# One diffusion-transformer step on one core: where the rows of the MLP norm come from, and which token tiles are paired for the MLP's operands

## The chip, the cores and the metric

The kernel runs on one core of one Trainium2 chip. The metric is device time in microseconds, median of three runs. PE is the matmul engine (TensorE), PEld its weight load, DVE VectorE, ACT ScalarE, POOL GpSimd, SP SyncE; all DMAs of this kernel are issued by SP, on one queue.

## The reference

One layer over 17 token tiles of 128 tokens: tile 0 is the context (128 tokens), tiles 1 to 16 are the latent tokens (2048). D is 1024, the MLP is 4096 wide.

```python
def block(x, s0, mod, ...):
    sh1, sc1, ga1, sh2, sc2, ga2 = mod
    h = rmsnorm(x, norm_mix_l) * (1.0 + sc1) + sh1
    o, s_new = mixer(h, s0, ...)          # projections, two-way delta scan, gMLP, w_out
    x = x + ga1 * o
    h = rmsnorm(x, norm_ffn_l) * (1.0 + sc2) + sh2
    x = x + ga2 * (jnp.square(jax.nn.relu(h @ w_ff1_l)) @ w_ff2_l)
    return x, s_new
```

The block runs once for the context (with `c_ctx`) and once for the latent tokens (with `c`); a last RMSNorm follows. The change is about the second norm: from `x` after the mixer to the operands of `h @ w_ff1_l`. All arithmetic is float32: each matmul operand is split into a rounded high part and a low part, and three matmuls make one product (`mm3`, lines 213 to 219).

## The kernel before

There are four stages in order of time: projections and convolution (to about 450 us); the scans over 34 units of one tile and direction (to about 1320); the first MLP matmul (to about 2370); the second.

**The backward scan** is a list of events with times in units (one unit is one tile's scan step). For tile t at unit i, `o_steps` (from line 1238) ends with the projection by w_out, adds the residual into two SBUF tiles `u["x"]` (lines 1293 to 1295), and stores them to the DRAM tensor `x2_d` (line 1296). Tiles 16 to 9 then run `h2_steps` (line 799) here, at offsets 3.17 to 3.71 (norm and transposes) and 3.71 to 4.71 (operands) from the list `WINDOWS`.

**`h2_steps(t)`** gives a list of steps:
- `norm2`: loads the tile's rows from `x2_d` (line 809), squares them on ACT with a running sum (811), DVE adds the sums, `rsqrt_cols` takes DVE and then POOL (175, 176), DVE scales the rows (815).
- `trans2(half)`: four PE transposes (822), then ACT applies the modulation (825) into `ev`; tiles named in `h2_d` are stored to DRAM (828).
- Tiles 4 to 1 and 12 to 9 go on: `partner` loads the stored `ev` of tile t + 4 as `y` (836), and `plain`, `third`, `fifth`, `sixth`, `fourth` form seven operands from the quarters of the pair (a fast 2 x 2 block scheme with seven products; the differences are line 849). `put` splits each into high part (ACT, 843) and low part (DVE, 844) and stores both to `hop_d` (846).

**The first MLP matmul** has two halves, g = 0 for tiles 9 to 16 and g = 1 for tiles 1 to 8 and 0. A half has 16 units of 256 hidden columns; a unit has seven products (`ORDER` = 1, 5, 6, 7, 3, 2, 4), and each product (a "step", position p in `seq`) is 12 matmuls of 512 columns against a resident operand tile (`hop`, 1 MB). Units 0 and 1, 14 and 15, 16 and 17 are interleaved product by product. In g = 1 tile 0's products come in as 128-column matmuls. With 112 steps in the first half, position 112 (`half`) starts the second.

At each p the program asks, in this order, for: the raw weights of the unit of step p + 10 (`loads_at(p + LEAD + 4)`, line 1445, four DMAs of 256 KB); the split weights of step p + 6 (`weights_at`, lines 1415 and 1421, made on DVE and ACT); the steps of `later` that are due; the products and their results (`step`, from line 1486), which ACT or DVE takes out of PSUM and SP stores to `z_d` (1481) and `s1_d`, `s2_d` (1484). `later` holds the `h2_steps` of tiles 8 to 0, 51 steps from p = 8 on at even distances of 90/51 = 1.76. `first_tile` (at p = 104) loads tile 0's `h2_d` (1554) and splits it right away on ACT and DVE. `hop_next` (893) loads the next operand tile; at p = 99, 101, ..., 111 (each step of unit 15) it loads one for the second half, into the buffer whose last reader is that step.

**Buffers and order.** Most tiles of 512 columns come from one pool `wp` of 49 (`w512`). The framework orders each engine's instructions by program order and by a planner's own model of time, hands out buffers as they come free in that model, and puts in the waits. At run time each engine, SP too, works its list in that order and stops at the first instruction whose wait isn't met.

Of the kernel before, what the change touches and what calls it, by code (L numbers as in the profile page):

```python
# [8 lines left out]
F32 = mybir.dt.float32  # L9
# [8 lines left out]
P = 128  # L18
# [43 lines left out]
def hybrid_step(  # L62
# [17 lines left out]
    def cond(t):  # L80
        return 0 if t == 0 else 1
# [20 lines left out]
    gate_d = dp.tile([NTOK, 512], F32, name="gate_d")  # L102
    ob_d = dp.tile([NTOK, 512], F32, name="ob_d")
    x2_d = dp.tile([NTOK, D], F32, name="x2_d")
    h2_d = {t: dp.tile([P, KT, P], F32, name=f"h2_{t}_d") for t in (0, 5, 6, 7, 8, 13, 14, 15, 16)}
    hop_d = {(g, o): dp.tile([P, 4, 2, 512], F32, name=f"hop_{g}_{o}_d") for g in range(2) for o in range(1, 8)}
    z_d = [dp.tile([4 if a else 1, P, 2, NK, P], F32, name=f"z{a}_d") for a in range(5)]
    s1_d, s2_d = ([dp.tile([4, P, NK, P], F32, name=f"s{i}{g}_d") for g in range(2)] for i in (1, 2))
# [95 lines left out]
    def w512(name):  # L204
        return wp.tile([P, 512], F32, tag="w", name=name)

    def wrow(row):

# [587 lines left out]

    bs = vec[:, 69:73]

    def h2_steps(t, psum, tmp, wide=w512):

        u = {}
        cd = cond(t)

        def norm2():
            u["x"] = x = [wide("x"), wide("x")]
            ss = smp.tile([P, 2], F32, tag="ss2", name="ss2")
            r = smp.tile([P, 1], F32, tag="r", name="r")
            for n in range(2):
                load(out=x[n], in_=x2_d[t * P : (t + 1) * P, n * 512 : (n + 1) * 512])
                junk = tmp()  # L810
                A.activation(junk, x[n], AF.Square, accum_out=ss[:, n : n + 1])
            V.tensor_tensor(out=ss[:, 0:1], in0=ss[:, 0:1], in1=ss[:, 1:2], op=ALU.add)
            rsqrt_cols(r, ss[:, 0:1], 1, 1.0 / D, EPS)
            for n in range(2):
                V.tensor_scalar_mul(x[n], x[n], r)

        def trans2(half):
            def f():
                ps = psum()
                ev = wide("ev")  # L820
                for i in range(4):
                    T.transpose(ps[:, i * P : (i + 1) * P], u["x"][half][:, i * P : (i + 1) * P], ident)
# [10 lines left out]
        def partner():  # L833
            u["y"] = [wide("y"), wide("y")]
            for half, y in enumerate(u["y"]):
                load(out=y.rearrange("p (k d) -> p k d", k=4), in_=h2_d[t + 4][:, half * 4 : half * 4 + 4, :])

        def put(o, src):

            dst = hop_d[t <= 8, o][:, :, :, (t - 1) % 4 * P : (t - 1) % 4 * P + P]  # L840
            h = wp.tile([P, 512], F32R, tag="w", name="opH")
            lo = wp.tile([P, 512], F32R, tag="w", name="opL")
            A.copy(h, src)
            V.tensor_tensor(out=lo, in0=src, in1=f32(h), op=ALU.subtract)
            for i, part in enumerate((h, lo)):
                store(out=dst[:, :, i, :], in_=f32(part).rearrange("p (k d) -> p k d", k=4))

        def sub(a, b, out=None):
            V.tensor_tensor(out=a if out is None else out, in0=a, in1=b, op=ALU.subtract)

        def plain():
            put(1, u[0])
            put(2, u[1])

        def third():
            put(3, u["y"][1])
            d = wide("d")
            sub(u["y"][1], u["y"][0], d)
            put(7, d)

        def fifth():
            sub(u["y"][0], u[0])
            put(5, u["y"][0])

        def sixth():
            sub(u["y"][1], u["y"][0])
            put(6, u["y"][1])

        def fourth():
            sub(u[1], u["y"][1])  # L870
            put(4, u[1])

        ops = [] if t in h2_d else [partner, plain, third, fifth, sixth, fourth]
        return [norm2, trans2(0), trans2(1)] + ops

    def sraw():
        return sp.tile([P, 512], F32, tag="raw", name="sraw")
# [18 lines left out]
    with ExitStack() as ph:  # L896
# [321 lines left out]
        def fraw():  # L1218
            return fp.tile([P, 512], F32, tag="gw", name="fraw")


        WO = []

# [14 lines left out]
        def o_steps(du):  # L1238
# [41 lines left out]
            def proj(n, k0):  # L1280
                def f():
                    if k0 == 0:
                        u["ps"] = pj()
                    for k in (k0, k0 + 1):
                        mm3(u["ps"], [(u["H"][k], u["L"][k]) + WO[n][k]], first=k == 0,
                            last=k == KT - 1)
                    if k0 == KT - 2:
                        sl = slice(n * 512, (n + 1) * 512)
                        tmp = fp.tile([P, 512], F32, tag="ug" if n else "vg", name="tmp")
                        ga = ga1[n]  # L1290
                        if cond(t) == 0:
                            ga = wrow(mod_d[0:1, 2 * D + n * 512 : 2 * D + n * 512 + 512])
                        x = u["x"][n]
                        V.tensor_tensor(out=tmp, in0=u["ps"], in1=ga, op=ALU.mult)
                        V.tensor_tensor(out=x, in0=x, in1=tmp, op=ALU.add)
                        store(out=x2_d[t * P : (t + 1) * P, sl], in_=x)
                return f

# [35 lines left out]
        for i, u in enumerate(units):  # L1334
            w = p2 if i <= NT else p3
            at(i - 3 if i > PL else -10, u["prep_loads"])
            at(i - 1, u["scan_loads"])
            n = len(u["prep"])
            for j, st in enumerate(u["prep"]):
                at(i - w[0] + (j + 0.5) * (w[0] - w[1]) / n, st, "prep")  # L1340
            spread(i + w[2], i + w[3], [scan_step(i, f) for f in u["scan"]], "chain")
            if i in (0, NT):
                at(i + w[2] + (w[3] - w[2]) * 0.7, lambda i=i: after(i))
            if i >= NT:
                at(i, lambda u=u: o_loads(u))
                first, second = o_steps(u)
                spread(i + p3[4], i + p3[5], first, "fill")
                spread(i + p3[6], i + p3[7], second, "fill")
                if u["t"] > 8:
                    st = h2_steps(u["t"], pj, fraw)  # L1350
                    spread(i + p3[8], i + p3[9], st[:3], "fill")
                    spread(i + p3[9], i + p3[9] + 1, st[3:], None)
        f2 = [f2_steps(t) for t in range(NT)]
        flat = []
        for n, (t, gi) in enumerate([(t, "g") for t in range(HT)] + [(t, gi) for t in range(HT) for gi in "vu"]
# [76 lines left out]
    class Unit:  # L1432
# [45 lines left out]
                first=onto is None, more=onto is not None)  # L1478

        def out(self, i, th, z):  # L1480
            store(out=z_d[(4, 2)[self.g] - 1 + th][:, :, i, self.jp, :].rearrange("a p d -> p a d"), in_=as4(z))

        def keep(self, dst, z):
            store(out=dst[self.g][:, :, self.jp, :].rearrange("a p d -> p a d"), in_=as4(z))
# [72 lines left out]
            x0[1].append(lo)  # L1557


    pairs = [(9 + i, 13 + i) for i in range(4)] + [(1 + i, 5 + i) for i in range(4)]  # L1560
    y0 = {}
    acc = {}
    kept = {}
# [56 lines left out]
    def s_parts(i, u, q):  # L1620

        ks = slice(4 * q, 4 * q + 4)

        def z(t, h):
            return z_d[(t + 3) // 4][(t - 1) % 4 if t else 0, :, h, ks, :]

        if u == 8:
            return {1: lambda: ([z(0, 0)],), 7: lambda: ([z(0, 0)],), 3: lambda: ([z(0, 0), z(0, 1)], ALU.add),
                    2: lambda: ([z(0, 1)],)}[i]()
        a, b = pairs[u]  # L1630
        g, m = divmod(u, 4)
        return {1: lambda: ([z(a, 0)],),
                5: lambda: ([s1_d[g][m, :, ks, :]],),
                6: lambda: ([s2_d[g][m, :, ks, :]],),
                7: lambda: ([z(a, 0), z(b, 0)], ALU.subtract),
                3: lambda: ([z(a, 1), s2_d[g][m, :, ks, :]], ALU.subtract),
                4: lambda: ([z(b, 1)],),
                2: lambda: ([z(a, 1)],)}[i]()
# [125 lines left out]
            begun.add(seq[p][1])  # L1764
            units[seq[p][1]].loads()

    for p in range(LEAD):
        loads_at(p)
    for p in range(LEAD):
        if p < 5:  # L1770
            hop_next()
        weights_at(p)
    later = [st for t in range(8, -1, -1) for st in h2_steps(t, bank, lambda: w512("junk"), w512)]
    n0 = len(seq) // 2 - 14
    later = [(8 + j * (n0 - 16) // len(later), st) for j, st in enumerate(later)]
    half = [p for p, e in enumerate(seq) if e[1] == NP][0]
    last = len(seq) - 16
    ps0 = None
    for p, (o, n, b) in enumerate(seq):
        u = units[n]  # L1780
        loads_at(p + LEAD + 4)
        weights_at(p + LEAD)
        while later and later[0][0] <= p:
            later.pop(0)[1]()
        if p == half - 8:
            first_tile()
        if o:
            u.step(o)
        if u.g:
# [108 lines left out]
```

## Time and profile before

| what | value |
|---|---|
| median of three runs (lowest, highest) | 2788.17 us (2787.95, 2789.26) |
| profiled execution | 2800.44 us |
| its span | 2798.7 us |
| its mean granted TensorE clock | 0.977 |
| DMA traffic | 585.10 MB, mean 209 GB/s |
| chain that ended last | PE 75%, DMA 10%, DVE 9%, issue 2%, ACT 2% |

In profile lines, `out<-in` names the tiles, `xN` is a count, L217 to L219 are the three matmuls of `mm3`, and a bracket at a line's end is the engine's idle time before the instruction and what ended it. A line of the waits reads: who waited, for whom, us in total, times, longest. The granted clock is the share of full speed that the chip allowed TensorE; 0.50 is half speed.

### The profile page before, as it was taken

The numbers are of one execution on the slowest core, as the hardware profiler recorded it, in microseconds if no ns is written. First come the engines' busy times: TensorE is split into PE (matmuls) and PEld (weight loads), VectorE is DVE, ScalarE is ACT, GpSimd is POOL, SyncE is SP. The second block draws the span as 40 slices with busy tenths as digits, with TensorE's granted clock in tenths as the row PEclk, the third lists the DMA queues.
The fourth block names the chain that finished last, engine by engine and source line by source line (L and its number), as shares of the span: only waits on it lengthen the run. The fifth ranks groups of instructions, "written<-read, shape, count | busy, mean of one in ns | idle before, by whom it ended". The sixth has DMA issues, their size and how long they took to land.

```text
span 2798.7 us, 45208 instructions
## 1 busy us (share of the span) xinstructions
PE 2655.7 (95%) x15698; PEld 2209.5 (79%) x15698; DVE 1869.1 (67%) x3909; ACT 1246.6 (45%) x3092; POOL 232.7 (8%) x448
## 2 busy tenths in 40 slices
PE   8999998999999899899798887999999999999998
PEld 4999996778887777778677776888888787788887
DVE  5867656777777878775467664655565555775874
ACT  4655555555555567653344442223342341332441
POOL 3111113111111111100000000000000000000000
PEclk9999999999999999899999898999999999999999
DMA  8866649555455667884758667433459997876682
GB/s 288 272 196 211 194 145 279 169 151 167 147 170 166 200 201 242 267 255 169 249 163 235 177 206 275 121 107 114 119 158 308 336 330 239 305 228 228 220 258 97
DMA packets 571691, 585.10 MB, mean 209 GB/s; under 512 B 35948, under 2 KB 401948, under 8 KB 567878
## 3 DMA queue, kind: packets, MB, share of 16 engines
q1 hardware_dynamic: 571462, 582.22, 65.4%
q8 instruction: 123, 2.02, 0.3%
q14 instruction: 106, 0.87, 0.1%
HBM read 402.34 MB, written 179.74 MB: 208 GB/s over the span
## 4 chain that ended last, share of the span: by engine, by line
PE 75%; DMA 10%; DVE 9%; issue 2%; ACT 2%; SPq 1%; POOL 1%; DVEq 0%; POOLq 0%; ACTq 0%
PE f L217 14%; PE f L219 14%; PE f L218 14%; PE pj L217 6%; PE pj L219 5%; PE pj L218 5%; PE pd L943 2%; DMA x<-x_d 2%; DMA qT<-qT_d 2%; PE pm L217 1%; PE pm L219 1%; PE pm L218 1%; PE pd L1120 1%; PE pt L568 1%; PE pd L1121 1%
## 5 line engine op out<-in xcount | busy, mean ns | idle before, releaser
L217 PE MATMUL f<-hop,wH 128*128 128x512 f32 x896 | 361.1, 404 | 52.6 <-ACT x L1491 21.6
L219 PE MATMUL f<-hop,zL 128*128 128x512 f32 x960 | 377.0, 393 | 1.8 <-DVE zL L1415 1.8
L217 PE MATMUL f<-hop,zH 128*128 128x512 f32 x960 | 376.7, 393 | 1.9 <-ACT zH L1421 1.9
L218 PE MATMUL f<-hop,zH 128*128 128x512 f32 x960 | 377.0, 393 | 0.0
L218 PE MATMUL f<-hop,wH 128*128 128x512 f32 x896 | 355.9, 397 | 0.0
L219 PE MATMUL f<-hop,wL 128*128 128x512 f32 x896 | 355.3, 397 | 0.0
L1421 ACT CAST zH<-zraw 128x512 fp32r<-128x512 f32 x240 | 147.0, 620 | 292.6 <-DVE zraw L1415 85.8
L217 PEld LDWEIGHTS f<-hop,wH 128*128 128x128 f32 x896 | 171.8, 192 | 90.7 <-ACT x L1491 22.4
L217 PEld LDWEIGHTS f<-hop,zH 128*128 128x128 f32 x960 | 180.4, 188 | 45.5 <-ACT zH L1421 2.7
L219 PEld LDWEIGHTS f<-hop,zL 128*128 128x128 f32 x960 | 180.3, 188 | 44.9 <-DVE zL L1415 2.6
L218 PEld LDWEIGHTS f<-hop,zH 128*128 128x128 f32 x960 | 180.2, 188 | 40.9
L1415 DVE TENSOR_TENSOR zL<-zraw,zH 128x512 fp32r<-128x512 f32 x240 | 162.8, 687 | 70.8 <-ACT zH L1421 54.2
L219 PEld LDWEIGHTS f<-hop,wL 128*128 128x128 f32 x896 | 171.5, 191 | 38.9
L218 PEld LDWEIGHTS f<-hop,wH 128*128 128x128 f32 x896 | 172.0, 192 | 35.8
L217 PE MATMUL pj<-kH,wH 128*128 128x386 f32 (+2 forms) x568 | 190.6, 338 | 0.3 <-DVE kH L466 0.3
L219 PE MATMUL pj<-kH,wL 128*128 128x386 f32 (+2 forms) x568 | 190.2, 335 | 0.0
L218 PE MATMUL pj<-kL,wH 128*128 128x386 f32 (+2 forms) x568 | 189.5, 334 | 0.0
L176 POOL TENSOR_TENSOR r<-rsq,nhalf 128x1 f32<-128x1 f32 (+1 forms) x38 | 26.3, 692 | 1575.4 <-DVE rsq L175 1575.4
L1415 DVE TENSOR_TENSOR wL<-raw,wH 128x512 fp32r<-128x512 f32 x112 | 76.4, 688 | 80.3 <-ACT wH L1421 79.3
L516 DVE SCALAR_TENSOR_TENSOR cv<-pj,vec,cv 128x384 f32<-128x384 f32 (+2 forms) x164 | 87.2, 539 | 59.4 <-ACT cv L513 57.9
L217 PEld LDWEIGHTS pj<-kH,wH 128*128 128x128 f32 x568 | 107.2, 189 | 4.9 <-issue 4.4
L217 PE MATMUL pj<-wH,hH 128*128 128x512 f32 x248 | 110.4, 445 | 0.0
(398 smaller groups left out, 6117.0 us busy)
## 6 DMA issues: line engine op xcount, KB each, us to landing
zraw<-z_d SPq DMA_DIRECT2D x212, 256.0 KB
raw<-in_w_ff_dram SPq DMA_DIRECT2D x128, 256.0 KB
hop<-hop_d SPq DMA_DIRECT2D x28, 1024.0 KB
z_d<-c SPq DMA_DIRECT2D x96, 256.0 KB
zraw<-s_d SPq DMA_DIRECT2D x96, 256.0 KB
raw<-in_w_mod_dram SPq DMA_DIRECT2D x80, 256.0 KB
r<-in_w_ff_dram SPq DMA_DIRECT2D x80, 256.0 KB
x<-x_d SPq DMA_DIRECT2D x68, 256.0 KB
```

The costliest lines, as they stand in the source:

```text
L176: G.tensor_tensor(out=out, in0=t[:np_, :n], in1=nhalf[:np_, :n], op=ALU.pow)
L217: T.matmul(ps, lh, rh, start=first and i == 0, stop=False, skip_group_check=more)
L218: T.matmul(ps, lh, rl, start=False, stop=False, skip_group_check=more)
L219: T.matmul(ps, ll, rh, start=False, stop=last and i == n - 1, skip_group_check=more)
L516: V.scalar_tensor_tensor(out=cv[:, o : o + m], in0=ps[:, s + sh : s + sh + m], scalar=convw[:, w, j : j + 1], in1=cv[:, o : o + m], op0=AL ...
L568: T.matmul(ps[:, i * P : (i + 1) * P], kTt[:, i * P : (i + 1) * P], rhs[:, i * P : (i + 1) * P], start=True, stop=True)
L943: T.matmul(p[:, h, :], lhs[:, h, :], rhs[:, h, :], start=True, stop=True)
L1120: T.matmul(p[:, h, :], u["qT"][:, h, :], s[:, h, :], start=True, stop=False)
L1121: T.matmul(p[:, h, :], u["QK"][:, h, :], u["vn"][:, h, :], start=s is None, stop=True)
L1415: V.tensor_tensor(out=out, in0=a, in1=b, op=op)
L1421: A.copy(h, src)
```

## The change

1. In `h2_steps`, loading (`rows`), `squares`, the reciprocal root (`norm2`) and scaling (`scale2`) become steps of their own. The partner's load moves into `squares`.
2. For tiles 8 to 0 `rows` is placed three steps ahead of the tile's position p = 10 + 19j/2 (j = 0 for tile 8), and the k-th further step at p + k. So rows are asked for at p - 3, squares come at p + 1, transposes at p + 4 and p + 5, operands of odd tiles at p + 6 to p + 10.
3. For tiles 16 to 9 there are no `rows`: `squares` takes the SBUF tiles that `o_steps` made. The offsets become 3.17 to 3.91, and 3.91 to 5.81 for operands.
4. Pairs are (t, t + 1) with t odd, where they were (t, t + 4). Operands are made for 15, 13, 11, 9 and 7, 5, 3, 1. The layouts of `hop_d`, `z_d` and `pairs` follow.
5. In the scan, `y` and `d` come from a new pool of five, the high and low parts from the four `raw` staging buffers.
6. Raw weights are asked for at p + 14 where it was p + 10; `first_tile` moves from 104 to 102; `hop_next` from 99, 101, ..., 111 to 101, 103, ..., 113.

```diff
-    h2_d = {t: dp.tile([P, KT, P], F32, name=f"h2_{t}_d") for t in (0, 5, 6, 7, 8, 13, 14, 15, 16)}
+    h2_d = {t: dp.tile([P, KT, P], F32, name=f"h2_{t}_d") for t in range(0, NT, 2)}
...
-    def h2_steps(t, psum, tmp, wide=w512):
+    def h2_steps(t, psum, tmp, wide=w512, part=None, half=None, src=None):
...
+        wide, part, half = wide, part or wide, half or w512
+
+        def rows():
+            u["x"] = [wide("x"), wide("x")]
+            for n in range(2):
+                load(out=u["x"][n], in_=x2_d[t * P : (t + 1) * P, n * 512 : (n + 1) * 512])
+
+        def squares():
+            if src:
+                u["x"] = src()
+            u["ss"] = smp.tile([P, 2], F32, tag="ss2", name="ss2")
+            for n in range(2):
+                A.activation(tmp(), u["x"][n], AF.Square, accum_out=u["ss"][:, n : n + 1])
+            if t % 2:
+                u["y"] = [part("y"), part("y")]
+                for h, y in enumerate(u["y"]):
+                    load(out=y.rearrange("p (k d) -> p k d", k=4), in_=h2_d[t + 1][:, h * 4 : h * 4 + 4, :])
 
         def norm2():
-            u["x"] = x = [wide("x"), wide("x")]
...
+            u["r"] = smp.tile([P, 1], F32, tag="r", name="r")
+            V.tensor_tensor(out=u["ss"][:, 0:1], in0=u["ss"][:, 0:1], in1=u["ss"][:, 1:2], op=ALU.add)
+            rsqrt_cols(u["r"], u["ss"][:, 0:1], 1, 1.0 / D, EPS)
+
+        def scale2():
             for n in range(2):
-                load(out=x[n], in_=x2_d[t * P : (t + 1) * P, n * 512 : (n + 1) * 512])
...
+                V.tensor_scalar_mul(u["x"][n], u["x"][n], u["r"])
...
-            dst = hop_d[t <= 8, o][:, :, :, (t - 1) % 4 * P : (t - 1) % 4 * P + P]
-            h = wp.tile([P, 512], F32R, tag="w", name="opH")
-            lo = wp.tile([P, 512], F32R, tag="w", name="opL")
+            c = (t - 1) % 8 // 2 * P
+            dst = hop_d[t <= 8, o][:, :, :, c : c + P]
+            h, lo = half("opH", F32R), half("opL", F32R)
...
-        ops = [] if t in h2_d else [partner, plain, third, fifth, sixth, fourth]
-        return [norm2, trans2(0), trans2(1)] + ops
+        ops = [plain, third, fifth, sixth, fourth] if t % 2 else []
+        return ([] if src else [rows]) + [squares, norm2, scale2, trans2(0), trans2(1)] + ops
...
+        def fpart(name):
+            return fp.tile([P, 512], F32, tag="part", name=name, bufs=5)
+
+        def fhalf(name, dt):
+            return sp.tile([P, 512], dt, tag="raw", name=name)
...
+                        du["x2"] = u["x"]
                         store(out=x2_d[t * P : (t + 1) * P, sl], in_=x)
...
-                    st = h2_steps(u["t"], pj, fraw)
-                    spread(i + p3[8], i + p3[9], st[:3], "fill")
-                    spread(i + p3[9], i + p3[9] + 1, st[3:], None)
+                    st = h2_steps(u["t"], pj, fraw, w512, fpart, fhalf, lambda u=u: u["x2"])
+                    spread(i + p3[8], i + p3[9] + 0.2, st[:5], "fill")
+                    spread(i + p3[9] + 0.2, i + p3[9] + 2.1, st[5:], None)
...
-    pairs = [(9 + i, 13 + i) for i in range(4)] + [(1 + i, 5 + i) for i in range(4)]
+    pairs = [(9 + 2 * i, 10 + 2 * i) for i in range(4)] + [(1 + 2 * i, 2 + 2 * i) for i in range(4)]
...
-    later = [st for t in range(8, -1, -1) for st in h2_steps(t, bank, lambda: w512("junk"), w512)]
-    n0 = len(seq) // 2 - 14
-    later = [(8 + j * (n0 - 16) // len(later), st) for j, st in enumerate(later)]
     half = [p for p, e in enumerate(seq) if e[1] == NP][0]
+    later = []
+    for j, t in enumerate(range(8, -1, -1)):
+        st = h2_steps(t, bank, lambda: w512("junk"), w512)
+        p = 10 + 19 * j // 2
+        later += [(p - (3 if k == 0 else 0) + k, st[k]) for k in range(len(st))]
+    later.sort(key=lambda e: e[0])
...
-        loads_at(p + LEAD + 4)
+        loads_at(p + LEAD + 8)
...
-        if p == half - 8:
+        if p == half - 10:
             first_tile()
...
-        if n == NP - 1:
+        if half - 11 <= p < half + 3 and (half - p) % 2:
             hop_next()
```

More of the change, by code (lines that the diff above doesn't have):

```diff
@@ L202, in load_w2, with w512 @@
         W2[gi].append(load_split(w_in[0, k * P : (k + 1) * P, off : off + 512]))
-    def w512(name):
-        return wp.tile([P, 512], F32, tag="w", name=name)
+    def w512(name, dt=F32):
+        return wp.tile([P, 512], dt, tag="w", name=name)
     def wrow(row):
@@ L797, in hybrid_step @@
     bs = vec[:, 69:73]
-    def h2_steps(t, psum, tmp, wide=w512):
+    def h2_steps(t, psum, tmp, wide=w512, part=None, half=None, src=None):
         u = {}
         cd = cond(t)
+        wide, part, half = wide, part or wide, half or w512
[13 more added lines that the diff above has]
+                    load(out=y.rearrange("p (k d) -> p k d", k=4), in_=h2_d[t + 1][:, h * 4 : h * 4 + 4, :])
         def norm2():
-            u["x"] = x = [wide("x"), wide("x")]
-            ss = smp.tile([P, 2], F32, tag="ss2", name="ss2")
-            r = smp.tile([P, 1], F32, tag="r", name="r")
+            u["r"] = smp.tile([P, 1], F32, tag="r", name="r")
+            V.tensor_tensor(out=u["ss"][:, 0:1], in0=u["ss"][:, 0:1], in1=u["ss"][:, 1:2], op=ALU.add)
+            rsqrt_cols(u["r"], u["ss"][:, 0:1], 1, 1.0 / D, EPS)
+        def scale2():
             for n in range(2):
[L809 to L815, printed above, removed]
+                V.tensor_scalar_mul(u["x"][n], u["x"][n], u["r"])
         def trans2(half):
@@ L831, in trans2 @@
             return f
[L833 to L836, printed above, removed]
         def put(o, src):
-            dst = hop_d[t <= 8, o][:, :, :, (t - 1) % 4 * P : (t - 1) % 4 * P + P]
-            h = wp.tile([P, 512], F32R, tag="w", name="opH")
-            lo = wp.tile([P, 512], F32R, tag="w", name="opL")
+            c = (t - 1) % 8 // 2 * P
+            dst = hop_d[t <= 8, o][:, :, :, c : c + P]
+            h, lo = half("opH", F32R), half("opL", F32R)
             A.copy(h, src)
             V.tensor_tensor(out=lo, in0=src, in1=f32(h), op=ALU.subtract)
-            for i, part in enumerate((h, lo)):
-                store(out=dst[:, :, i, :], in_=f32(part).rearrange("p (k d) -> p k d", k=4))
+            for i, piece in enumerate((h, lo)):
+                store(out=dst[:, :, i, :], in_=f32(piece).rearrange("p (k d) -> p k d", k=4))
         def sub(a, b, out=None):
@@ L856, in third @@
             put(3, u["y"][1])
-            d = wide("d")
+            d = part("d")
             sub(u["y"][1], u["y"][0], d)
@@ L1480, in out @@
         def out(self, i, th, z):
-            store(out=z_d[(4, 2)[self.g] - 1 + th][:, :, i, self.jp, :].rearrange("a p d -> p a d"), in_=as4(z))
+            store(out=z_d[(3, 1)[self.g] + th][:, :, i, self.jp, :].rearrange("a p d -> p a d"), in_=as4(z))
         def keep(self, dst, z):
@@ L1624, in z @@
         def z(t, h):
-            return z_d[(t + 3) // 4][(t - 1) % 4 if t else 0, :, h, ks, :]
+            if t == 0:
+                return z_d[0][0, :, h, ks, :]
+            return z_d[1 + 2 * (t > 8) + (t - 1) % 2][(t - 1) % 8 // 2, :, h, ks, :]
         if u == 8:
@@ L1765, in loads_at @@
             units[seq[p][1]].loads()
-    for p in range(LEAD):
+    for p in range(LEAD + 8):
         loads_at(p)
```

## The prediction

> **What bounds the kernel now.** I read the page's first table, then the engines' busy time by stretch, then who waited for whom in the stretch that loses, and last the order of time around its three longest stalls.
>
> ```profile
> PE 2655.7 (95%) x15698; PEld 2209.5 (79%) x15698; DVE 1869.1 (67%) x3909; ACT 1246.6 (45%) x3092; POOL 232.7 (8%) x448
> ...
> 1323.00:1715.00 392.00, 322.98 (x1380) 261.41 (x1378) 231.00 (x384) 152.93 (x318) 7.44 (x9) 0.92 0.71 222
> 1750.00:2142.00 392.00, 392.00 (x2090) 335.50 (x2089) 236.77 (x375) 125.32 (x229) 0.00 (x0) 1.00 0.47 140
> ...
> 1000.00:1110.00 110.00, 107.31 (x946) 87.29 (x945) 88.46 (x234) 78.95 (x247) 17.69 (x22) 1.00 0.71 223
> 1110.00:1220.00 110.00, 92.01 (x685) 75.05 (x683) 90.85 (x217) 66.28 (x190) 16.59 (x19) 0.88 0.90 276
> ```
>
> A stretch row gives its length, then busy PE, PEld, DVE, ACT, POOL, then granted clock, DMA share and GB/s. PE is the bound. It is without a gap in the second MLP half (1750 to 2142), but idle 69.0 us in the first (1323 to 1715), which runs the norm of tiles 8 to 0 between its products. The only other loss of size is 18.0 us at 1110 to 1220, where the scan makes its operands.
>
> ```profile
> PE f L217 <- ACT x L1491: 21.6, 2, 15.1
> PE f L217 <- ACT p L1502: 21.1, 2, 18.3
> PE f L822 <- DVE x L815: 16.4, 3, 8.4
> PE f L217 <- ACT p L1495: 10.0, 2, 8.6
> ...
> ACT junk L811 <- DMA x<-x_d: 46.7, 13, 11.4
> ACT wH L1421 <- DVE s L1415: 43.9, 18, 8.2
> ...
> ACT x0H L1421 <- DMA x<-h_d: 36.1, 2, 21.1
> ```
>
> These four PE waits (1350 to 1750) are the 69 us, in nine gaps. PE waits for ordinary ACT copies and for the scaled rows; ACT in its turn stands for 46.7 us before the squares of line 811, until rows read from x2_d land, and for 36.1 us before the cast of tile 0.
>
> ```profile
> 1645.50 0.81 SPq L809 DMA_DIRECT2D x<-x_d  x1
> ...
> 1647.19 0.50 SPq L809 DMA_DIRECT2D x<-x_d  x1
> ...
> 1649.78 0.63 ACT L811 ACTIVATE junk<-x 128x512 f32<-128x512 f32 x1 [11.44 <-DMA x<-x_d]
> ...
> 1692.00 5.57 SPq L893 DMA_DIRECT2D hop<-hop_d  x6
> 1697.63 0.41 SPq L1554 DMA_DIRECT2D x<-h_d  x1
> ...
> 1713.87 0.62 ACT L1421 CAST x0H<-x 128x512 fp32r<-128x512 f32 x1 [14.95 <-DMA x<-h_d]
> ...
> 1715.03 0.80 PE L217 MATMUL f<-hop,wH 128*128 128x512 f32 x1 [18.28 <-ACT p L1502]
> ```
>
> Both stalls have one form: a load, and directly behind it on ACT the instruction that needs it, so that all later copies queue behind a transfer. At 1697.63 the transfer itself stands behind three hop tiles of 1 MB.
>
> ```profile
> 1489.40:1492.80 3.40, 3.40 (x8) 2.72 (x9) 3.40 (x7) 0.62 (x1) 1.04 (x1) 0.50 0.36 90
> ...
> sum 68.10, PE 31.15 PEld 24.77 DVE 31.57 ACT 21.14 POOL 4.54; mean PE 4.45 PEld 3.54 DVE 4.51 ACT 3.02 POOL 0.65
> ...
> sum 27.20, PE 25.29 PEld 21.71 DVE 22.71 ACT 15.52 POOL 5.83; mean PE 4.22 PEld 3.62 DVE 3.79 ACT 2.59 POOL 0.97
> ```
>
> The first sum is over the seven stretches between 1369 and 1719 whose granted clock is 0.50, the second over the six between 1117 and 1220. PE worked 31.15 and 25.29 us at half speed, and half of that is lost: 15.6 and 12.6 us. So the first MLP half loses 69.1 + 15.6 = 84.7 us, the operand stretch 18.0 + 12.6 = 30.6 us.
>
> **The change part by part: rows of tiles 8 to 0.** A step of the MLP order is 12 matmuls:
>
> ```profile
> 1328.53 0.59 ACT L1495 COPY p<-f 128x512 f32<-128x512 f32 x1 [1.70 <-PE f L219]
> 1331.33 0.59 ACT L1495 COPY p<-f 128x512 f32<-128x512 f32 x1 [1.70 <-PE f L219]
> ...
> 1146.92 4.92 DMA x<-x_d
> ```
>
> Two copies behind consecutive products are 2.80 us apart. Before, load, squares and scaling were issued in one step and the transposes 1.76 steps (4.9 us) later. After, the rows are issued four steps (11.2 us) ahead of the squares and transposed three steps after those. A row load took 4.92 us where the DMA share was highest; 6 us are left for SP to be late. Squares, sum, POOL's power and scaling get a step (2.80 us) each, more than any lasts. So I let the 50.8 us of gaps that are not tile 0's go, with their clock, and ask what is late next.
>
> ```profile
> 1334.04 14.83 SPq L1445 DMA_DIRECT2D raw<-in_w_ff_dram  x4
> ...
> 1352.76 0.62 ACT L1421 CAST wH<-raw 128x512 fp32r<-128x512 f32 x1 [9.93 <-DMA raw<-in_w_ff_dram]
> ```
>
> First, the start. Unit 2's weights are queued right behind five hop tiles whether asked for at step 4 or, now, at step 0, so ACT's 9.93 us wait stays, and its backlog is part of the 15.1 us gap that follows; I leave 5 us idle and 2 of clock. Later units gain four steps on their weight loads. Second, operand making. It costs the same work as before:
>
> ```profile
> L844 DVE TENSOR_TENSOR opL<-ev,opH x24: 678/684/1115, 1101.3 to 1638.7; 128x512 fp32r<-128x512 f32 x24
> ...
> L849 DVE TENSOR_TENSOR d<-y x8: 677/686/689, 1107.4 to 1623.0; 128x512 f32<-128x512 f32 x8
> ```
>
> Seven low parts and four differences are 7.5 us of DVE for each of four odd tiles, but in five consecutive steps (14 us) instead of 8.8. The stretch row gives DVE 231 us; without 30 for operands 201/112 = 1.8 us a step remain, so a burst needs 5 x 1.8 + 7.5 = 16.5 us in 14. DVE falls 2.5 us behind; weights are made six steps ahead, which covers it; the bare lag if not. I leave 1.5 us a burst and 2 of clock together: 8. On average DVE is at 231/325 = 71%.
>
> The pool of 49 tiles has to hold more: by my count 8 raw weights (5 before), 14 split weights, 1 sum, some 6 results, and 11 of the norm at its worst, 40 together. Cost nothing while that is under 49. Per unit SP issues as many DMAs as before; the same 222 GB/s x 392 us go into some 325 us, 268 GB/s, which the stretch 1110:1220 exceeded.
>
> **Tile 0 and the hop tiles.** Tile 0's load moves from step 104 to 102, the second-half hop loads from step 99 to 101 and on. Before, three hops precede it in the program, now one, for whose buffer SP waits only until step 99. PE ran on for some six steps without ACT before its 18.28 us stop, so a 10 us wait on ACT should be hidden. I leave 3 us of 18.28 + 1.5 (clock); if the planner again puts hop loads ahead of tile 0's second half, all 20 stay. The hop of step 112 is asked for 11 steps (31 us) ahead, and its landing stays covered.
>
> Together: 7 + 8 + 3 = 18 us remain of 84.7; gain 67. Bounds: 85 if nothing remains; 33 if half of the row gaps and their clock (32) and all of tile 0's (20) stay.
>
> **The scan.** For tiles 16 to 9 the 16 row loads go. Operand making for 12, 11, 10, 9 in one unit each becomes 15, 13, 11, 9 over 1.9 units each, from about 1020 instead of 1099.
>
> ```profile
> 1039.36 0.62 ACT L811 ACTIVATE fraw<-x 128x512 f32<-128x512 f32 x1
> ...
> 1060.71 0.63 ACT L811 ACTIVATE fraw<-x 128x512 f32<-128x512 f32 x1
> ...
> ACT fraw L811 <- DMA x<-x_d: 9.2, 6, 2.1
> ...
> ACT opH L843 <- DMA hop_d<-opH: 4.6, 2, 2.7
> ```
>
> A unit is 21.4 us by these two squares of neighbouring tiles. The 9.2 us of ACT waits for rows go. The high and low parts now come from four buffers, not from the pool of 49, so a cast can wait for a store two products back, as the 4.6 us show; operand steps are 0.38 units (8 us) apart, against 4.9 us for a transfer, so this should hide. DVE is what may not: two tiles' work, 15 us, moves into 1000:1110, where it was busy 88.5 of 110 and becomes 94%, with the scan's short matmuls waiting for each result. Upper bound: all 30.6 us come back. Lower: the moved half brings its half of that loss, 15 us, and the rest keeps its own. I take a gain of 12, under half of the loss, because that DVE share lies nearer to the stretch that loses than to the one that does not.
>
> **Sum.** 67 + 12 = 79 us. The profiled execution took 2800.44 us (span 2798.7), 12.3 over the median 2788.17; I subtract from both: 2721 profiled, **2709** median.
>
> [...]
>
> **The rivals.**
> - *Tile 0 still late* (0.12): hop loads again precede its second load, as at 1692.00. Against: the program now has one hop ahead of it. 2709 + 17 = 2726.
> - *Rows still late* (0.10): SP issues in order, and rows wait behind stores whose data is late, or transfers lengthen in the denser stage; lead 11.2 us, transfer 4.92, so SP must be over 6 us late. For it: 14.83 us for four issues at the start. Half of the row loss, 32 us, stays: 2741.
> [...]
> - *Scan saturated* (0.08): DVE at 94% costs 15 instead of saving 12: 2736.
> - *Nothing moves* (0.04): the planner sets the squares right behind the loads again; the scan then gives little: within 5 us of 2788.
> - *Slower* (0.06): the pool runs over 49 live tiles because rows and weights are held longer. Then each unit's weights arrive late, as unit 2's did (9.93 us on ACT); lateness in every unit uses up the six steps' lead and reaches PE: 14 units x 9.9 = 139 us, 2848. It decides from ten tiles more than I count.
>
> **How the numbers follow.** The forecast (remainders as above, within some 20 us) has 0.60. The bounds of the parts give 85 + 31 = 116 us (2672) and 33 - 15 = 18 (2770). Both extremes need all parts to agree; the range 2688 to 2764 takes in the first three rivals and leaves out those two ends, the unmoved and the slower case. A measurement of this kernel can tell 0.2% (5.6 us) from no change. Faster: 0.60 + 0.12 + 0.10 + 0.08 = 0.90; same 0.04; slower 0.06.
>
> **What would show it.** Right: squares of line 811's successor in the first MLP half wait almost nothing for x2_d; PE's idle there near 14 us, its clock 0.98; no gap over 5 us before the second half; granted clock above 0.93 at 1110 to 1220. Wrong: ACT waiting for first-layer weights in every unit (pool), PE waiting for DVE's P and S at 1000 to 1110 (scan), or a gap over 10 us before the first product of the second half (tile 0).

## The result, and the profile after

| | before | after |
|---|---|---|
| median (lowest, highest), us | 2788.06 (2784.34, 2789.26), 4 runs | 2707.5 (2706.15, 2716.66), 4 runs |
| profiled execution, us | 2800.44 | 2707.53 |
| its mean granted clock | 0.977 | 0.990 |

The ratio is 0.972, 95% interval 0.9697 to 0.9743: 2.8% faster, 80.6 us between the medians. The forecast was 2709. Two executions of the experiments, e5's profiled one (4320.44 us, granted clock 0.555) and one of e6's (9167.53 us), ran in a disturbed, slow state and are in no median, ratio or stage below.

The page's first table, and six stretches by engine, of after (columns as in the prediction: length, busy PE, PEld, DVE, ACT, POOL, clock, DMA share, GB/s):

```profile
PE 2632.3 (97%) x15698; PEld 2196.5 (81%) x15698; DVE 1868.0 (69%) x3909; ACT 1246.1 (46%) x3092; POOL 228.2 (8%) x448
```

```profile
1303.00:1642.00 339.00, 326.11 (x1454) 266.64 (x1453) 248.66 (x416) 157.81 (x328) 5.64 (x9) 0.98 0.83 261
1503.00:1506.40 3.40, 3.23 (x10) 2.75 (x11) 3.37 (x7) 1.50 (x4) 0.00 (x0) 0.51 1.05 286
1615.60:1622.40 6.80, 4.44 (x11) 3.37 (x12) 4.98 (x9) 4.18 (x8) 0.00 (x0) 0.50 0.59 245
1066.00:1069.40 3.40, 3.40 (x14) 2.43 (x10) 2.14 (x4) 1.43 (x4) 0.00 (x0) 0.51 0.00 0
...
1000.00:1110.00 110.00, 99.93 (x858) 80.77 (x857) 92.33 (x232) 79.50 (x245) 18.83 (x23) 0.98 0.81 257
1110.00:1220.00 110.00, 104.13 (x917) 85.55 (x916) 94.66 (x236) 70.83 (x215) 14.81 (x17) 1.00 0.79 255
```

The first MLP half is idle on PE for 339.0 - 326.1 = 12.9 us, where it was 69.0, at clock 0.98; the second and third row are its half-speed stretches (at 1619 us one matmul of 512 columns follows another every 0.43 us, at 1611 every 0.23). The same bytes now come at 261 GB/s (estimate 268). In the scan the loss is not gone but shared out: 1110 to 1220 lost 18.0 us and now 5.9; 1000 to 1110 lost 2.7 and now 10.1. The clock gained more: 1110 to 1220 ran at 0.88 and now runs at 1.00.

Who waited for whom in after, 1330 to 1660, PE and then ACT:

```profile
PE f L836 <- DVE x L829: 7.1, 3, 5.0
PE f L217 <- ACT wH L1437: 5.8, 1, 5.8
```

```profile
ACT wH L1437 <- DVE s L1431: 56.3, 22, 8.3
...
ACT x0H L1437 <- issue: 11.8, 1, 11.8
ACT x0H L1437 <- DMA x<-h_d: 10.1, 1, 10.1
```

In after, L809 loads the rows, L816 squares, L829 scales, L836 transposes; L1431, L1437, L1507 and L1511 are the old L1415, L1421, L1491 and L1495. ACT's 46.7 us of waiting for x2_d are gone, and what ACT waits for longest is now DVE's sums for the weights (56.3 us). PE waits four times in all: three times for rows that DVE scales, and once, behind tile 0's casts on ACT, for a cast of weights.

To separate the stages I use two rows of the trace that give the first and the last start of a group. One group is the sums of forward and backward scan (17 in the backward scan), the other the ACT copy of product 1 (32 in the first MLP matmul). Before, before again (experiment e0), and after:

```profile
L1127 DVE TENSOR_TENSOR o<-pd,of x17: 679/691/693, 925.1 to 1297.6; 128x512 f32<-128x512 f32 x17
...
L1491 ACT COPY x<-f x32: 575/588/606, 1322.9 to 2074.3; 128x512 f32<-128x512 f32 x32
```

```profile
L1127 DVE TENSOR_TENSOR o<-pd,of x17: 678/691/692, 922.9 to 1288.5; 128x512 f32<-128x512 f32 x17
...
L1491 ACT COPY x<-f x32: 573/588/605, 1313.8 to 2062.3; 128x512 f32<-128x512 f32 x32
```

```profile
L1136 DVE TENSOR_TENSOR o<-pd,of x17: 681/685/692, 917.4 to 1272.3; 128x512 f32<-128x512 f32 x17
...
L1507 ACT COPY x<-f x32: 565/588/621, 1297.7 to 1980.6; 128x512 f32<-128x512 f32 x32
```

| stretch, us | before | before again | after |
|---|---|---|---|
| backward scan | 372.5 | 365.6 | 354.9 |
| first MLP matmul | 751.4 | 748.5 | 682.9 |

Against the two profiles of before, the first MLP matmul is 65.6 to 68.5 us shorter and the scan 10.7 to 17.6. The forecast had 67 and 12.

### The profile page after: what moved, and what is told of

Its sections match the earlier page's. It is cut to its first block, busy times and chain, and to the rows that moved or that the text cites. A ratio compares the mean times of both kernels' runs of the same rounds, so it can differ in the third digit from the quotient of the medians.

```text
span 2705.8 us, 45189 instructions
## 1 busy us (share of the span) xinstructions
PE 2632.3 (97%) x15698; PEld 2196.5 (81%) x15698; DVE 1868.0 (69%) x3909; ACT 1246.1 (46%) x3092; POOL 228.2 (8%) x448
## 4 chain that ended last, share of the span: by engine, by line
PE 82%; DMA 7%; DVE 6%; issue 2%; ACT 2%; SPq 1%; POOL 0%; DVEq 0%; POOLq 0%; ACTq 0%
PE f L219 16%; PE f L217 16%; PE f L218 16%; PE pj L217 6%; PE pj L219 6%; PE pj L218 6%; PE pd L952 3%; PE pm L217 1%; DMA qT<-qT_d 1%; PE pm L218 1%; PE pm L219 1%; PE pt L568 1%; PE pd L1129 1%; PE pd L1130 1%; PE pt L528 1%
## 5 line engine op out<-in xcount | busy, mean ns | idle before, releaser
L217 PE MATMUL f<-hop,wH 128*128 128x512 f32 x896 | 356.2, 398 | 5.8 <-ACT wH L1437 5.8
L218 PE MATMUL f<-hop,wH 128*128 128x512 f32 x896 | 352.0, 393 | 0.0
L1437 ACT CAST zH<-zraw 128x512 fp32r<-128x512 f32 x240 | 147.1, 620 | 299.2 <-DVE zraw L1431 91.9
L1431 DVE TENSOR_TENSOR zL<-zraw,zH 128x512 fp32r<-128x512 f32 x240 | 162.6, 687 | 68.2 <-ACT zH L1437 50.8
L1431 DVE TENSOR_TENSOR wL<-raw,wH 128x512 fp32r<-128x512 f32 x112 | 76.1, 687 | 76.0 <-ACT wH L1437 75.0
```

The source lines that it names most:

```text
L217: T.matmul(ps, lh, rh, start=first and i == 0, stop=False, skip_group_check=more)
L218: T.matmul(ps, lh, rl, start=False, stop=False, skip_group_check=more)
L1431: V.tensor_tensor(out=out, in0=a, in1=b, op=op)
```

## The experiments

The stage rows are a finer measure than the medians. Two other kernels below have the first MLP matmul's program in common with after (e6, e9) and a third adds held buffers alone (e8): 681.5 to 684.1 us with after's own 682.9. Six others share after's scan program (e1, e2, e3, e4, e8, e11): 352.3 to 357.0 us. The two profiles of before differ by 2.9 us in the first stage and by 6.9 in the scan. So 3 us tell in the first stage, while in the scan a single profile tells little under 7 us. Intervals of the ratio are some 5 us wide to either side. Each ratio below is to the kernel before, on the same chip; for comparison, after has 0.972 (0.9697 to 0.9743).

| kernel | edit to after | median us | ratio (95%) | scan | first MLP matmul |
|---|---|---|---|---|---|
| e0_before | (before itself) | 2788.62, one run | | 365.6 | 748.5 |
| e1_rows_late | no lead for rows | 2756.48 | 0.9866 (0.985 to 0.9883) | 354.9 | 737.2 |
| e2_norm_tight | norm in one step | 2736.81 | 0.9798 (0.9784 to 0.9813) | 354.1 | 709.4 |
| e3_tile0_old | tile 0, hops at old steps | 2709.88 | 0.9703 (0.9686 to 0.972) | 357.0 | 679.4 |
| e4_loads_old | weight loads 4 steps later | 2720.45 | 0.975 (0.9736 to 0.9765) | 352.3 | 694.3 |
| e5_scan_reload | rows reloaded in the scan | 2713.37, three runs | 0.9727 (0.9711 to 0.9743) | | |
| e6_scan_dense | operands in 1 unit | 2709.7, three runs | 0.9719 (0.97 to 0.9739) | 359.1 | 684.1 |
| e7_old_pairs | pairs t, t + 4 | 2706.05 | 0.9698 (0.9684 to 0.9713) | 349.2 | 682.6 |
| e8_hold | 9 tiles of the pool held | 2713.38 | 0.9718 (0.9699 to 0.9737) | 354.7 | 682.7 |
| e9_scan_wp | scan operands from the pool of 49 | 2718.05 | 0.9733 (0.9712 to 0.9754) | 362.9 | 681.5 |
| e10_old_pairs_dense | e6 and e7 together | 2713.61 | 0.9723 (0.9706 to 0.974) | 360.3 | 684.4 |
| e11_best | see below | 2694.77 | 0.9654 (0.9637 to 0.9671) | 356.2 | 668.3 |

**e0: the kernel before, profiled again.**

> The kernel before, profiled a second time. Its first profiled execution was 2800.44 us, 12.3 over the median; the kernel after was profiled at its median. Theory: the 12 us were one execution's, spread over stages that the change does not touch, so this profile shows a span near 2787, the same nine PE gaps of 69 us (within 8) in the first MLP half, and the scan reaching its middle some 8 us earlier than in the first profile. Rival: profiling itself costs this kernel 12 us; then the span is near 2799 again.

It took 2788.62 us, and its nine PE gaps come to 68.3 us, as expected. The 12 us by which the prediction's profile stood over the median were that execution's own, but they don't lie where I had put them: 7 us are in the scan and 3 in the first MLP matmul, stages that the change does touch.

**e1 and e2: what the rows needed.** The line that places the steps of tiles 8 to 0, in after, e1 and e2:

```diff
-        later += [(p - (3 if k == 0 else 0) + k, st[k]) for k in range(len(st))]
+        later += [(p + max(k, 1), st[k]) for k in range(len(st))]                            # e1
+        later += [(p - 3 if k == 0 else p + 3 if k < 4 else p + k, st[k]) for k in range(len(st))]   # e2
```

> The rows of tiles 8 to 0 are asked for in the same step as their squares (no lead); all else as after. Theory (the lead matters: a load directly ahead of its reader on ACT blocks every copy behind it): most of the first MLP half's gain goes, 35 to 60 us slower, 2743 to 2767, with ACT waiting 40 us or more for x2_d. Rival (what matters is that squares, sum, scaling and transposes each have a step of their own, so that PE's transposes come late enough): under 10 us slower.

> The rows keep their lead, but squares, sum with root and scaling fall into one step, directly ahead of the transposes' step; all else as after. Theory (the lead matters): within 8 us of after, 2700 to 2716, a few short waits of PE for the scaled rows. Rival (the spacing matters): PE waits for scaled rows at most tiles, 2 to 4 us each with half-speed time, 20 us or more slower.

ACT's longest wait in e1, and the stage row of e1:

```profile
ACT junk L816 <- DMA x<-x_d: 66.4, 11, 15.4
```

```profile
L1507 ACT COPY x<-f x32: 566/588/627, 1302.3 to 2039.5; 128x512 f32<-128x512 f32 x32
```

In e1 the theory held. Without lead the stage is 737.2 us, 54 longer, and ACT stands 66.4 us before the squares again: the median is 49 us over after's, inside 35 to 60. In e2 the theory failed and the rival held: with lead but without spacing the stage loses 26.5 us and the median 29, where "within 8" was expected. Its PE waits, 1300 to 1750:

```profile
PE f L836 <- DVE x L829: 17.0, 6, 5.6
PE f L217 <- ACT wH L1437: 5.0, 1, 5.0
PE f L217 <- ACT x L1507: 3.0, 1, 3.0
```

Here ACT has no wait for x2_d left. PE's transposes come up before the chain of squares (ACT), sum (DVE), root (POOL) and scaling (DVE), with DVE's weights and results in between, has delivered the scaled rows. Lead takes the transfer out of ACT's list, spacing takes that chain out of PE's. Neither does the other's work.

**e3 and e4: tile 0 and the weight loads.**

```diff
-        if p == half - 10:
+        if p == half - 8:                                              # e3
-        if half - 11 <= p < half + 3 and (half - p) % 2:
+        if n == NP - 1:                                                # e3
-        loads_at(p + LEAD + 8)
+        loads_at(p + LEAD + 4)                                         # e4
```

> Tile 0's load and the second half's hop loads are put back to their old steps (104; 99, 101 to 111); all else as after. Theory: the gap before the second half, 5.8 us in after, grows back to 14 to 18 us, 8 to 14 us slower, 2716 to 2722. Rival: the planner's order of hop loads and tile 0's second load, not the two steps, sets this gap, and the time stays within 4 us of after.

> Raw weights of the first MLP matmul are asked for four steps later again (p + 10); all else as after. Theory 1 (this lead adds little in the middle of the half): within 5 us of after, 2703 to 2713. Theory 2 (it is this lead, not the two steps of tile 0, that shortened the gap before the second half from 18 to 6 us, since the eight raw loads no longer stand between the hop loads and tile 0): that gap is over 12 us again and the time 8 to 15 us longer.

PE's waits in e3 and in e4 (1300 to 1750 and to 1660), then ACT's wait for weights in e4:

```profile
PE f L836 <- DVE x L829: 7.1, 3, 5.0
PE f L217 <- ACT p L1518: 2.7, 1, 2.7
```

```profile
PE f L836 <- DVE x L829: 15.2, 3, 8.3
PE f L217 <- ACT wH L1437: 5.9, 1, 5.9
```

```profile
ACT wH L1437 <- DMA raw<-in_w_ff_dram: 12.2, 2, 10.0
```

In e3 the gap before the second half did not grow back but is 2.7 us, and the stage is 3.5 us shorter than after's: moving tile 0 and the hop loads gained nothing. In e4 that gap is 5.9 us, not over 12, so theory 2 falls with e3's theory, and theory 1 (within 5 us) falls by e4's time. What e4 loses, 11.4 us in the stage, is at its start: ACT waits 10.0 us for a unit's weights again, and PE 8.3 us for the first scaled rows behind it. SP's issues at the start of the stage, in after and then in e4, show why:

```profile
1292.36 2.10 SPq L1461 DMA_DIRECT2D raw<-in_w_ff_dram  x4
...
1296.70 8.86 SPq L902 DMA_DIRECT2D hop<-hop_d  x10
```

```profile
1298.60 8.63 SPq L902 DMA_DIRECT2D hop<-hop_d  x10
1310.55 14.86 SPq L1461 DMA_DIRECT2D raw<-in_w_ff_dram  x4
```

Asked for four steps earlier, the four loads of unit 2 are placed ahead of the hop loads; asked for at the old step, they stand behind all ten of them.

The gap before the second half shrank from 18.3 us with a change in the same list. In before, six hop loads stand between tile 0's two loads (the prediction's rows at 1692.00 and 1697.63), and ACT casts from the second one 16.2 us after its issue. In after, and then in e3, there are four:

```profile
1598.61 6.24 SPq L902 DMA_DIRECT2D hop<-hop_d  x4
1604.89 0.43 SPq L1570 DMA_DIRECT2D x<-h_d  x1
```

```profile
1603.07 6.24 SPq L902 DMA_DIRECT2D hop<-hop_d  x4
1609.35 0.65 SPq L1570 DMA_DIRECT2D x<-h_d  x1
```

Here ACT casts from it 11.9 and 11.6 us after its issue. (A hop tile is 2 MB, two loads of 1 MB each. The description and the prediction have 1 MB for a tile.) So e3's rival held: its time is 2.4 us over after's, and the planner's order, not the two steps, goes with the gap. What in the change made the planner order it so is left open: each of the two edits can be undone alone without bringing the old gap back, and undoing both was not tried.

**e5 to e7, e9, e10: the scan.**

```diff
-                    st = h2_steps(u["t"], pj, fraw, w512, fpart, fhalf, lambda u=u: u["x2"])
+                    st = h2_steps(u["t"], pj, fraw, w512, fpart, fhalf)                    # e5
+                    st[0:2] = [lambda a=st[0], b=st[1]: (a(), b())]                        # e5
+                    st = h2_steps(u["t"], pj, fraw, w512, None, None, lambda u=u: u["x2"]) # e9
-                    spread(i + p3[9] + 0.2, i + p3[9] + 2.1, st[5:], None)
+                    spread(i + p3[9] + 0.2, i + p3[9] + 1.2, st[5:], None)                 # e6, e10
```

e7 and e10 put back the old pairing:

```diff
-    pairs = [(9 + 2 * i, 10 + 2 * i) for i in range(4)] + [(1 + 2 * i, 2 + 2 * i) for i in range(4)]
+    pairs = [(9 + i, 13 + i) for i in range(4)] + [(1 + i, 5 + i) for i in range(4)]
-            if t % 2:
+            if t not in h2_d:      # the old set: 0, 5 to 8, 13 to 16
-                    load(..., in_=h2_d[t + 1][...])
+                    load(..., in_=h2_d[t + 4][...])
```

and the layouts of `hop_d` and `z_d` with it.

> In the scan, tiles 16 to 9 load their rows from x2_d again, in the step of the squares; pairing, spreading and the first MLP half as after. Theory: ACT waits some 10 us for rows there again, in short waits that hold up the scan's copies; MLP start 3 to 8 us later, 2711 to 2716. Rival (these waits were covered): within 2 us of after. Second rival: DMA share of the stage makes it 10 us or more.

> In the scan, the operands of tiles 15, 13, 11 and 9 are made within 1 unit instead of 1.9; all else as after. Theory (spreading is what saves time in the scan, DVE being over its share while operands are made in one unit): PE gaps and half-speed time at the four places, MLP start 8 to 20 us later, 2716 to 2728. Rival (making them only in every second unit is enough): within 4 us of after.

> Tiles t and t + 4 are paired again, with the operands made for 12, 11, 10, 9 and 4, 3, 2, 1; rows' lead, spaced norm steps, 1.9 units per tile in the scan and all else as after. Theory (pairing spreads the operand work over the whole stretch): the scan loses 10 to 20 us at its end again, and the first MLP half 5 to 15 us around tiles 4 to 1, where DVE needs 9.5 x 1.8 + 7.5 + 1.4 = 26 us in each 26.6; together 2720 to 2740. Rival (the lead and the spacing do it all): within 6 us of after.

> In the scan, the partner's rows, differences and high and low parts come from the pool of 49 again instead of the pool of five and the four staging buffers; all else as after. Neither the pairing nor the spreading alone made the scan quicker, and the reload explains 6 of its 16 us. Theory (buffers of their own are the rest, since casts waited for hop stores before): MLP start 6 to 12 us later, 2713 to 2720. Rival (it is pairing or spreading, each of which suffices alone): within 4 us of after.

> Old pairing and one unit per tile for the operands together, as before; no reload, own buffers and the first MLP half as after. Theory (pairing and spreading stand in for each other): the scan's end is dense again at four successive units, DVE and DMA over their share, MLP start 8 to 15 us later than in after, 2715 to 2725. Rival (own buffers are what counts): within 4 us of after.

e5's three runs, 2711.11 to 2719.08, lie within 3 us of what after's runs cover, so the reload's price is not settled, and the "6 us" in e9's expectation is only a difference of medians. The scan rows of e6, e7, e9 and e10, one for each kernel:

```profile
L1136 DVE TENSOR_TENSOR o<-pd,of x17: 680/685/692, 915.8 to 1274.9; 128x512 f32<-128x512 f32 x17
```

```profile
L1136 DVE TENSOR_TENSOR o<-pd,of x17: 679/686/692, 919.4 to 1268.6; 128x512 f32<-128x512 f32 x17
```

```profile
L1136 DVE TENSOR_TENSOR o<-pd,of x17: 678/683/692, 923.1 to 1286.0; 128x512 f32<-128x512 f32 x17
```

```profile
L1136 DVE TENSOR_TENSOR o<-pd,of x17: 680/690/692, 920.6 to 1280.9; 128x512 f32<-128x512 f32 x17
```

The new pairing is no gain: with the old one the scan is 349.2 us, below all seven profiles of after's scan program, and the median 2706.05 is within 2 us of after's; the 15 to 35 us that my theory expected are absent, in the MLP half as well (682.6). Making the operands in one unit instead of 1.9 costs 4 us with the new pairs (e6), too little to tell, and e6's time is within 4 us of after's, as its rival had it. With the old pairs it costs 11 (360.3 against 349.2, one profile each; the medians differ by 7.6), and e10's 2713.61 lies between its theory and its rival. With operands from the pool of 49, e9's scan is 362.9 us, 8 over after's and outside the range of its seven profiles, but that too is one profile, and its ratio's interval overlaps after's.

e9's time lies in the range of its theory, but its trace shows another cause than casts that wait for hop stores. ACT's casts and PE, 1000 to 1216, in after and then in e9:

```profile
ACT opH L852 <- DMA hop_d<-opH: 9.3, 7, 2.7
ACT fraw L816 <- DVE x L1310: 8.8, 3, 3.6
```

```profile
ACT opH L852 <- DMA hop_d<-opH: 3.6, 2, 1.9
...
PE pj L1286 <- DMA ob<-ob_d: 6.0, 3, 2.6
```

Casts wait less for hop stores with the large pool, not more. Instead PE waits 6.0 us for `ob`, a tile of the pool of 49 that the projection by w_out reads, and not at all in after. In e9, SP waits for hop stores before its loads into that pool, 12.3 us in the scan (910 to 1300): 7.0 for `x`, 3.6 for the forward scan's sums and the gate, 1.7 for `ob`. The two largest of these waits:

```profile
SPq L1282 <- DMA hop_d<-opL: 5.7, 3, 2.7
...
SPq L1251 <- DMA hop_d<-opL: 3.3, 2, 2.6
```

In after there is none of them. In before, PE's waits for `ob` are 3.7 us and in its second profile 2.0, so e9 says what the own buffers are worth beside the rest of the change, and not that before lost as much.

**e8: is the pool nearly full?** Nine tiles of the pool were allocated at the start of the first MLP half, written once and read at step 94:

```diff
+    held = [w512("held") for _ in range(9)]
+    for h in held:
+        V.memset(h[:, 0:1], 0.0)
...
+        if p == half - 18:
+            for h in held:
+                V.tensor_copy(h[:, 1:2], h[:, 0:1])
```

> After, with nine tiles of the pool of 49 held from the start of the first MLP half to step 94 (nine one-column writes and reads on DVE added). Theory (at most 40 tiles are live, so nine can be missed): within 5 us of after. Rival (the pool is nearly full): the first half's weights or rows come late, ACT waits for them in many units and the time is 15 us or more longer.

The stage took 682.7 us against 682.9, so nine tiles can be missed, as the count of at most 40 has it. The median's 6 us more lie ahead of the edit: the first copy of the stage starts at 1304.4, not 1297.7.

**e11: the two gaps that after still has.** One of them is DVE's lag, the other tile 0's load, on which ACT stands (10.1 us in its waits above) until just before the last row shown:

```profile
1497.84 0.68 DVE L853 TENSOR_TENSOR opL<-ev,opH 128x512 fp32r<-128x512 f32 x1
...
1501.57 0.15 DVE L824 TENSOR_TENSOR ss<-ss 128x1 f32<-128x1 f32 x1
...
1502.63 0.88 DVE L829 TENSOR_SCALAR x<-x,r 128x512 f32<-128x512 f32 x2 [0.72 <-POOL r L176]
1503.17 0.69 PE L836 MATMUL f<-ident,x 128*128 128x128 f32 x2 [5.00 <-DVE x L829]
...
1617.96 0.80 PE L217 MATMUL f<-hop,wH 128*128 128x512 f32 x1 [5.78 <-ACT wH L1437]
```

In these rows of after in order of time, DVE is still at the last low part of one tile's operands when PE is ready for the next tile's transposes; the scaling follows 4 us later, and PE has stood 5 us. e11 gives the transposes one more step and asks for tile 0 seven steps ahead of its split:

```diff
-        later += [(p - (3 if k == 0 else 0) + k, st[k]) for k in range(len(st))]
+        later += [(p - 3 if k == 0 else p + k + (k > 3), st[k]) for k in range(len(st))]
...
-        if p == half - 10:
-            first_tile()
+        if p == half - 15:
+            first_load()      # the two loads of first_tile alone
+        if p == half - 8:
+            first_tile()      # the splits alone
```

> After, with transposes and operands of tiles 8 to 0 one step later than the scaling (one more step for DVE's lag), and tile 0's load asked for at step 97, its split at 104. Theory: of after's four PE gaps in the first half (5.0 before transposes, 5.8 before the second half, 0.9 and 1.2) the first goes to under 2 and the second to under 3, with their half-speed time: 6 to 14 us faster than after, 2693 to 2701. Rival (the lag moves to the next reader of DVE's or ACT's results): within 3 us of after.

PE's waits in e11, 1300 to 1660, and its stage row:

```profile
PE f L836 <- DVE x L829: 1.3, 2, 1.0
PE f L217 <- ACT p L1518: 0.6, 1, 0.6
```

```profile
L1507 ACT COPY x<-f x32: 563/588/612, 1300.2 to 1968.5; 128x512 f32<-128x512 f32 x32
```

1.9 us of waiting are left of after's 12.9, the profiled execution's mean granted clock is 0.993 where after's is 0.990, and the stage is 14.6 us shorter. How much each of the two edits gave was not tried. The ratio to before, 0.9654 (0.9637 to 0.9671), lies below after's interval: this version beats both kernels, by some 99 us against before on the same chip (2793.41) and 13 us, median against median, against after.

## Why the prediction was right, point by point

- **What bounds, and the loss.** Right: nine gaps in the second profile of before too, and 65.6 to 68.5 us came back in the first MLP matmul for 67 forecast.
- **The sum is partly luck.** 18 us were to remain in the first MLP half: 7 at the start, 8 for bursts, 3 for tile 0. In after it is 0.9, 7.8 and 8.0 us, together 16.7: 12.9 us of gaps, and half of the 7.7 us that PE worked at half speed. The start came out 6 us better and tile 0 5 us worse, and the two errors nearly cancel.
- **Rows of tiles 8 to 0.** Right in direction and size together, but the prediction credited the lead and took the spacing for granted. e1 prices the lead at 54 us of the stage and e2 the spacing at 26.5. With e4's 11.4 they add up to 92, more than the whole gain: the three overlap, so they can't be read as shares of it.
- **"That wait stays" (unit 2's weights).** Wrong, in the faster direction: asking four steps earlier was argued to change nothing because the hop tiles stand ahead. The planner put the loads ahead of the hop tiles (1292.36 against 1296.70), and e4 loses 11.4 us of the stage without that.
- **Bursts of operand making.** 8 us were left, and 7.8 stayed: gaps of 5.0 and 1.2 us, and half of the 3.2 us of work in one half-speed stretch. The mechanism, DVE behind after five dense steps, is the one of the rows above.
- **Tile 0.** 3 us were left, and a gap of 5.8 with a half-speed stretch stayed, so the sign "no gap over 5 us before the second half" was missed too. The step that failed is the one that put the gain on steps 102 and 101: e3 has the old steps and the smaller gap.
- **The scan.** The size came out (12; measured 10.7 to 17.6, by which of before's two profiles one takes), its reason only in part. The 9.2 us of waits for rows did go, but the squares now wait 8.8 us for DVE's residual sum `x`. The casts' waits for hop stores grew from 4.6 to 9.3 us without a loss that shows. DVE rose in 1000 to 1110 from 88.5 us to 92.3, 84% of the stretch and not the 94% forecast, and PE lost 7.4 us there; the gain at 1110 to 1220 outweighs it. A sign of being wrong came in part: PE waits 10.8 us for DVE's `P` at 1000 to 1216, where it was 5.0. Pairing gains nothing; how far spreading, the reload or the operands' own buffers, priced at zero in the prediction, made the gain is not settled.
- **Rivals.** The pool rival is refuted by e8 as far as nine tiles go. "Rows still late" did not come: squares in the first MLP half wait for no row. "Scan saturated" did not come either (DVE 84% and 86% of the two stretches).

## What to carry to other kernels

A load and its first reader in one step put a transfer into the reader's whole list (66.4 us of ACT's waits in e1): ask steps ahead, and then also give each engine of the chain behind it a step of its own (without it, PE waited 17.0 us in e2), for the two remedies fix different waits. Look for the gain of a change with several edits by undoing them one at a time, and read the stage rather than the total: here the row of the first MLP matmul repeats to 3 us where the ratio needs 5 or more, while the scan's needs more than one profile. Read the queue's order in the profile after a change, for a load that is asked for earlier can land in another place of the list than the one expected (here unit 2's weights, at 1292.36 ahead of the hop loads at 1296.70). And look at the buffers of a side task as well as at its place: in e9, loads that had nothing to do with the operands waited 12.3 us for the operands' stores, and its scan took 362.9 us, where e6's, with the operands in one unit, took 359.1 and after's 354.9, one profile each.

## What was not expected of the hardware

PE's two gaps ahead of the half-speed stretch at 1066.00 of after (shown among the first stretches: 3.40 us, PE busy throughout, clock 0.51), and the one ahead of the stretch at 1489.40 of before:

```profile
1065.05 0.29 PE L1038 MATMUL pd<-P,X 128*128 128x64 f16 x4 [1.44 <-DVE P L1029]
1065.71 0.28 PE L1038 MATMUL pd<-P,X 128*128 128x64 f16 x4 [0.25 <-DVE P L1029]
```

```profile
1489.36 0.79 PE L217 MATMUL f<-hop,wH 128*128 128x512 f32 x1 [2.85 <-ACT p L1502]
```

(The first two rows are f16: the scan's small products are not float32, as the description has it.) The clock fell to half for 3.4 us after 1.69 us of idleness in two pieces, and after a single gap of 2.85 us. But it did not fall in the 9 us after a gap of 2.35 us in before, which came ahead of this row:

```profile
1360.88 0.33 PE L822 MATMUL f<-ident,x 128*128 128x128 f32 x1 [2.35 <-DVE x L815]
```

So the length of one gap alone does not decide it in these traces. The seven half-speed stretches in the first MLP half of before last 3.4, 6.8, 6.8, 10.2, 10.2, 13.6 and 17.1 us, about whole multiples of 3.4.
